# Eight k pairs instead of six in seven-product quads, with the first weight sum made by a negated copy and two adding transfers

## The chip, the core and the metric

The kernel runs on one core of a Trainium2 chip. Its engines are named here as the profile names them: PE (TensorE, matmul), PEld (TensorE's weight loads, which overlap PE), DVE (VectorE), ACT (ScalarE), POOL (GpSimd) and SP (SyncE, which issues most of the loads). The metric is the device time of one execution in microseconds; lower is better.

## The reference

One block of a network on 256 tokens of width 2048, in float32. It has three residual branches in a row: a gated feed-forward, a mixer (a recurrent RWKV part and a pooling part), and a second gated feed-forward. The change touches only the last matmul of the two feed-forwards.

```python
def _rmsnorm(x, g):
    y = x * lax.rsqrt(jnp.mean(x * x, axis=-1, keepdims=True) + NORM_EPS)
    return y * g

def _swiglu(x, w_gate, w_up, w_down):
    return (jax.nn.silu(x @ w_gate) * (x @ w_up)) @ w_down

f = _swiglu(_rmsnorm(h, ln_ffn1_pre), ffn1_gate, ffn1_up, ffn1_down)
h = h + 0.5 * _rmsnorm(f, ln_ffn1_post)
h = h + _rmsnorm(_hybrid_mixer(...), ln_mix_post)
f = _swiglu(_rmsnorm(h, ln_ffn2_pre), ffn2_gate, ffn2_up, ffn2_down)
h = h + 0.5 * _rmsnorm(f, ln_ffn2_post)
```

The down product `@ w_down` takes 256 x 5632 hidden values to 256 x 2048.

## The kernel before, in words

**Precision.** Every float32 operand is split in a rounded high part and a low part (`xH`, `xL` for activations, `wH`, `wL` for weights). One product of two blocks is three matmuls, in `mm3` (lines 156 to 160): high by high, low by high, high by low. A weight tile is 128 rows by 1024 values; ACT rounds it to `wH` (a cast) and DVE subtracts to get `wL`.

**Buffers.** A loaded tile `w32` has four buffers (`W32_BUFS`), `wH` and `wL` have five each (`WS_BUFS`). All larger temporary tiles share 33 units of 128 x 1024 values (`NUNITS`, `unit`, line 82). During a down product the 22 hidden activation tiles hold 22 of these units.

**The down product.** K is 5632, which is 44 blocks of 128 rows; the 2048 output columns are four chunks of 512. `post` (line 530) calls `seven` (line 235) twice per feed-forward, each time for two neighbouring chunks, called first (`cf`) and last (`cl`); so there are four calls in the kernel. Tokens are two halves of 128. A pair of neighbouring k blocks, two halves of tokens and two chunks of columns form a 2 x 2 by 2 x 2 product of blocks. In the plain form this takes eight products.

**Plain pairs.** `pair` (line 265) loads two k blocks of one chunk, 512 KB, splits them and makes four products. The call first runs over the plain pairs for the first chunk, then over those for the last one.

**Quads.** The first `NQ` = 6 k pairs, k blocks 0 to 11, are not done in the plain form, but each as one quad with seven products (`quad`, line 271; a Winograd form of Strassen's method). It needs sums of activation blocks and of weight blocks:

- `sums` (line 211) works on one activation tile, which covers two k pairs. DVE rebuilds x from `xH` and `xL` (the tile `sx`), makes four sums of its quarters (the tile `sf`), ACT rounds all four in one cast (`sH`, line 230) and DVE subtracts (`sL`, line 231). The results are kept and serve both calls of a feed-forward. The first `sums` stands ahead of the plain pairs; later ones are made inside the quads of the first call, ahead of need.
- The weights of a quad are loaded in two tiles `va` and `vb`, as four 256 KB transfers issued by SP (line 279). DVE makes the first weight sum, `t13`, as `va` minus a block of `vb` (line 283), and from it the two halves of `t24` (lines 285 and 286). In the trace both sums are called `t`. Four splits (lines 293 and 294) then give the high and low parts.

The seven products go to banks `p1`, `p5`, `p6`, `p7` (called `ms` in the trace) and `f0`, `l0`, `l1` (called `mm`). After the last quad `merge` (line 320) combines the four `ms` banks, and the first chunk is given out to be scaled and squared.

**Where the quads stand.** `QUADS` gives the plain pairs, counted from 0, behind which a quad is placed: for the first call (`False`) and the second one (`True`), each for the first chunk's pairs and the last chunk's. In the second call the last 16 k blocks of the last chunk are done token half by token half (`by_half`), so that one half can be finished while the other still computes.

**What sets the order.** A planner puts each engine's instructions in a fixed order by priority and by its own estimate of when their inputs are ready. Weight work is raised in priority (`high_priority` with `BOOST`). `sums` is not raised. At run time every engine and every queue works in that order, so an instruction that waits holds up all behind it. SP's queue issues the weight loads; POOL's queue issues the few other transfers around a down product: the broadcast gain `gb` (line 547), the residual (`xr` in the first feed-forward, `h` in the second, line 1297) and the spills.

**Just ahead of the first quad.** The last block of the up product ends in `shuffle_split` (line 485): sixteen ACT copies of 32 x 256 (line 493), a cast (line 496) and a DVE subtraction (line 497) give the last hidden tile.

Of the kernel before, what the change touches and what calls it, by code (L numbers as in the profile page):

```python
# [11 lines left out]
F32 = mybir.dt.float32  # L12
F32R = mybir.dt.float32r
AF = mybir.ActivationFunctionType
ALU = mybir.AluOpType
# [3 lines left out]
P = 128  # L19
# [24 lines left out]
TURNS = [[4.2, 5.3, 6.4, 7.5], [5.3, 6.0, 6.7, 7.4]]  # L44
WARM = 12
TB = 4
NQ = 6
QUADS = {False: ((4, 9, 14), (2, 5, 8)), True: ((2, 5, 8, 11, 14), (1,))}

ROWS = [("ln_mix_pre", 16), ("ln_ffn2_pre", 16), ("mu", 26), ("w0", 8), ("a0", 8),  # L50
        ("k_k", 8), ("k_a", 8)]
# [3 lines left out]
class Block:  # L55
# [41 lines left out]
    def at(s, t, fn):  # L97

        s.n += 1
        heapq.heappush(s.events, (t, s.n, fn))  # L100
# [109 lines left out]

    def sums(s, T, out):

        nc = s.nc
        V = nc.vector
        xH, xL = T[len(out) // 2]
        x = s.unit((P, 2, 2, S), F32, "sx")
        fl = lambda t: t.rearrange("p a b t -> p (a b t)")
        V.tensor_tensor(out=fl(x), in0=xH.bitcast(F32).rearrange("p k t -> p (k t)"),  # L218
                        in1=xL.bitcast(F32).rearrange("p k t -> p (k t)"), op=ALU.add)
        a11, a21 = x[:, :, 0, :P], x[:, :, 0, P:]  # L220
        a12, a22 = x[:, :, 1, :P], x[:, :, 1, P:]
        f = s.unit((P, 4, 2, P), F32, "sf")
        V.scalar_tensor_tensor(out=f[:, 0], in0=a21, scalar=-1.0, in1=a22, op0=ALU.mult,
                               op1=ALU.subtract)
        V.scalar_tensor_tensor(out=f[:, 1], in0=f[:, 0], scalar=-1.0, in1=a11,
                               op0=ALU.mult, op1=ALU.subtract)
        V.tensor_tensor(out=f[:, 2], in0=a11, in1=a21, op=ALU.subtract)
        V.tensor_tensor(out=f[:, 3], in0=a12, in1=f[:, 1], op=ALU.subtract)
        fH, fL = [s.unit((P, 4, 2, P), F32R, n_) for n_ in ("sH", "sL")]
        nc.scalar.copy(fl(fH), fl(f))  # L230
        V.tensor_tensor(out=fl(fL), in0=fl(f), in1=fl(fH).bitcast(F32), op=ALU.subtract)
        for i in range(2):
            out.append([(fH[:, m, i], fL[:, m, i]) for m in range(4)])

    def seven(s, w, cf, cl, at, KT, T, sm, ev_first, ev_last, trail):


        nc = s.nc
        V = nc.vector
        n = NQ  # L240
        K0 = 2 * n

        bank = {}
        for b in ("f0", "f1", "l0", "l1"):
            bank[b] = s.pm.tile([P, 512], F32, tag="mm", name=s.nm("mm"))
        for b in ("p1", "p5", "p6", "p7"):
            bank[b] = s.psum("ms")
        std = KT - K0
        left = dict(f0=std + n, f1=std, l0=std + n, l1=std + n, p1=n, p5=n, p6=n, p7=n)
        new = set(bank)  # L250

        def mul(b, x, wt):
            left[b] -= 1
            s.mm3(bank[b], *x, *wt, b in new, left[b] == 0)
            new.discard(b)

        def rows(k, h):
            xH, xL = at(k)
            return xH[:, h * P:h * P + P], xL[:, h * P:h * P + P]
        ws = {}  # L260

        def keep(tiles):
            ws.update((k, (wH, wL)) for k, wH, wL in tiles)

        def pair(k, c0, b):
            keep(s.load_w(w, k, 2, c0, 512))
            for i in range(2):
                for h in range(2):
                    mul(f"{b}{h}", rows(k + i, h), ws[k + i])

        def quad(q):
            k = 2 * q
            if len(sm) < min(q + 2, n):
                s.sums(T, sm)
            va, vb = [s.wp.tile([P, 1024], F32, tag="w32", name=s.nm("w32"), bufs=W32_BUFS)
                      .rearrange("p (a c) -> p a c", a=2) for _ in range(2)]
            for dst, kk, c0 in ((va[:, 0], k, cl), (vb[:, 0], k, cf), (va[:, 1], k + 1, cf),
                                (vb[:, 1], k + 1, cl)):
                nc.sync.dma_start(out=dst, in_=w[kk * P:kk * P + P, c0:c0 + 512])
            t13 = s.unit((P, 2, 512), F32, "t13")  # L280
            t24 = s.unit((P, 2, 512), F32, "t24")
            with s.tc.high_priority(offset=BOOST):
                V.tensor_tensor(out=t13, in0=va,  # L283
                                in1=vb[:, :1].to_broadcast([P, 2, 512]), op=ALU.subtract)
                V.tensor_tensor(out=t24[:, 0], in0=va[:, 0], in1=t13[:, 1], op=ALU.add)
                V.tensor_tensor(out=t24[:, 1], in0=vb[:, 1], in1=t24[:, 0], op=ALU.subtract)  # L286

            def split(v, m):
                wH = s.wp.tile([P, 1024], F32R, tag="wH", name=s.nm("wH"), bufs=WS_BUFS)
                wL = s.wp.tile([P, 1024], F32R, tag="wL", name=s.nm("wL"), bufs=WS_BUFS)  # L290
                H, L = [t_[:, :m * 512].rearrange("p (a c) -> p a c", a=m) for t_ in (wH, wL)]
                with s.tc.high_priority(offset=BOOST):
                    nc.scalar.copy(H, v)  # L293
                    V.tensor_tensor(out=L, in0=v, in1=H.bitcast(F32), op=ALU.subtract)  # L294
                return [(H[:, i], L[:, i]) for i in range(m)]
            s1, s2, s3, s4 = sm[q]
            b11, b22 = split(va, 2)
            mul("p1", rows(k, 0), b11)
            mul("f0", s4, b22)
            b21, = split(vb[:, 1:], 1)  # L300
            mul("l0", rows(k + 1, 0), b21)
            t1, t3 = split(t13, 2)
            mul("p5", s1, t1)
            mul("p7", s3, t3)
            t2, t4 = split(t24, 2)
            mul("p6", s2, t2)
            mul("l1", rows(k + 1, 1), t4)

        if not sm:
            s.sums(T, sm)  # L310
        q = iter(range(n))
        stop = KT - (TRAIL if trail else 0)
        for i, k in enumerate(range(K0, KT, 2)):
            pair(k, cf, "f")
            if i in QUADS[trail][0]:
                quad(next(q))
        tiles = list(range(K0, stop, 2))
        u = [s.tmp("u") for _ in range(4)]

        def merge():  # L320
            with s.tc.high_priority(offset=BOOST):
                nc.scalar.copy(u[0], bank["p1"])
                for o, b, i in ((1, "p6", 0), (2, "p7", 1), (3, "p5", 2), (1, "p5", 1),
                                (1, "f0", 1), (3, "f1", 3)):
                    V.tensor_tensor(out=u[o], in0=bank[b], in1=u[i], op=ALU.add)
                ev_first(0, u[1])
                ev_first(1, u[3])

        def finish(h):
            o = u[2 * h]  # L330
            V.tensor_tensor(out=o, in0=bank[f"l{h}"], in1=o, op=ALU.add)
            ev_last(h, o)
        for i, k in enumerate(tiles):
            pair(k, cl, "l")
            if i in QUADS[trail][1]:
                quad(next(q))
                if left["p1"] == 0:
                    merge()
        if not trail:
            with s.tc.high_priority(offset=BOOST):  # L340
                finish(0)
                finish(1)
            return
        s.now = 0.0
        s.by_half(w, cl, stop, KT, 0.0, AHEAD[0],
                  lambda k, h: mul(f"l{h}", rows(k, h), ws[k]), keep, finish)
# [1007 lines left out]
```

## Time and profile before

| | us |
|---|---|
| median of three runs | 2102.93 (2102.6 to 2103.97) |
| the profiled execution | 2103.1 |
| its span, first to last instruction | 2101.4 |
| PE busy | 2077.6 |
| DVE busy | 1389.0 |
| ACT busy | 1157.0 |
| POOL busy | 76.0 |
| bytes moved | 406.99 MB |
| mean granted TensorE clock | 0.994 |
| down product of the first feed-forward | about 490 to 720 |
| down product of the second | about 1850 to 2085 |

A group or an instruction in the trace is written as line, engine, operation and output <- inputs; numbers in square brackets are the idle time of the engine just before it and what ended that. A matmul over 512 columns is shown as 0.39 us long, since its end overlaps the next one; back to back they start 0.2267 us apart at full clock. So it is the starts that tell the rate.

### The profile page before, as it was taken

Reading aid. Unit: us, or ns where it says so; the run is one execution under the profiler, and the core shown is the slowest. Engines: PE = TensorE matmul, PEld = TensorE weight load, DVE = VectorE, ACT = ScalarE, POOL = GpSimd, SP = SyncE. Lnnn points to the kernel's source line nnn. Section 1 sums busy time; section 2 is a strip of 40 time slices with the busy share of each in tenths; the row PEclk is TensorE's granted clock in tenths of the full one; section 3 lists DMA queues with packets and bytes.
Section 4 is the critical chain, followed back from the end, with each engine's and each line's share of the span. In section 5 each row is a group of like instructions: output and inputs, shape, how many; then the busy total and the mean of one; then the engine's idle time right before and its main releaser. Section 6 shows DMA issues by size and latency. Waiting matters only on the chain.

```text
span 2101.4 us, 29096 instructions
## 1 busy us (share of the span) xinstructions
PE 2077.6 (99%) x11017; PEld 1748.1 (83%) x11017; DVE 1389.0 (66%) x1776; ACT 1157.0 (55%) x1658; POOL 76.0 (4%) x161
## 2 busy tenths in 40 slices
PE   9999999999999999999999999999999999989998
PEld 7888888887888899999888788888888888878886
DVE  6555555556787765799688666575655555567776
ACT  7565555655555565474466444466555565555543
POOL 0000000000000010000110110010000000000000
PEclk9999999999999999999999999999999999999999
DMA  7656666564667666556456565565665656645674
GB/s 260 194 179 208 194 194 196 178 204 153 207 196 253 222 188 189 177 165 194 133 159 189 160 249 188 194 220 181 197 203 191 192 179 208 195 152 199 205 243 160
DMA packets 224885, 406.99 MB, mean 194 GB/s; under 512 B 13919, under 2 KB 49897, under 8 KB 224745
## 3 DMA queue, kind: packets, MB, share of 16 engines
q1 hardware_dynamic: 218569, 384.69, 57.3%
q0 software_dynamic: 5888, 19.93, 2.6%
q8 instruction: 86, 1.41, 0.3%
q10 hardware_dynamic: 288, 0.52, 0.1%
q14 instruction: 54, 0.44, 0.1%
HBM read 396.69 MB, written 8.39 MB: 193 GB/s over the span
## 4 chain that ended last, share of the span: by engine, by line
PE 95%; DVE 2%; issue 1%; ACT 1%; POOL 0%; DMA 0%; POOLq 0%; DVEq 0%; SPq 0%; ACTq 0%
PE mm L158 26%; PE mm L160 26%; PE mm L159 26%; PE mc L438 10%; PE ms L159 1%; PE ms L160 1%; PE ms L158 1%; ACT x L493 1%; PE tr L466 1%; PE pA L1075 0%; ACT wH L293 0%; PE pSa L1183 0%; DVE sx L218 0%; PE pU L1171 0%; DMA w<-in_ffn_gate_dram 0%
## 5 line engine op out<-in xcount | busy, mean ns | idle before, releaser
L135 DVE TENSOR_TENSOR wL<-w,wH 128x1024 fp32r<-128x1024 f32 (+2 forms) x677 | 811.0, 1209 | 546.2 <-ACT wH L134 542.9
L134 ACT CAST wH<-w 128x1024 fp32r<-128x1024 f32 (+2 forms) x677 | 698.7, 1044 | 634.2 <-PE mm L160 491.9
L160 PE MATMUL mm<-wH,xL 128*128 128x512 f32 x2316 | 902.2, 390 | 0.7 <-DVE xL L474 0.7
L159 PE MATMUL mm<-wL,xH 128*128 128x512 f32 x2316 | 902.0, 389 | 0.0
L158 PE MATMUL mm<-wH,xH 128*128 128x512 f32 x2316 | 897.9, 392 | 0.0
L160 PEld LDWEIGHTS mm<-wH,xL 128*128 128x128 f32 x2316 | 435.1, 188 | 92.4 <-DVE xL L474 1.5
L158 PEld LDWEIGHTS mm<-wH,xH 128*128 128x128 f32 x2316 | 435.7, 188 | 90.3 <-ACT xH L472 0.2
L159 PEld LDWEIGHTS mm<-wL,xH 128*128 128x128 f32 x2316 | 435.4, 188 | 89.5 <-DVE wL L135 0.2
L438 PE MATMUL mc<-xH,wH 128*128 128x256 f32 x560 | 159.5, 285 | 0.0
L438 PE MATMUL mc<-xL,wH 128*128 128x256 f32 x560 | 158.4, 283 | 0.0
L438 PE MATMUL mc<-xH,wL 128*128 128x256 f32 x560 | 158.3, 283 | 0.0
L493 ACT COPY x<-T 32x256 f32<-32x256 f32 x352 | 141.9, 403 | 3.9
L438 PEld LDWEIGHTS mc<-xH,wH 128*128 128x128 f32 x560 | 106.0, 189 | 1.1
L438 PEld LDWEIGHTS mc<-xH,wL 128*128 128x128 f32 x560 | 106.0, 189 | 0.2
L438 PEld LDWEIGHTS mc<-xL,wH 128*128 128x128 f32 x560 | 106.0, 189 | 0.1
L293 ACT CAST wH<-t 128x1024 fp32r<-128x1024 f32 x48 | 50.5, 1051 | 63.0 <-DVE t L286 31.0
L293 ACT CAST wH<-w 128x1024 fp32r<-128x1024 f32 (+1 forms) x48 | 40.2, 838 | 63.7 <-DMA w<-in_ffn_down_dram 45.6
L294 DVE TENSOR_TENSOR wL<-t,wH 128x1024 fp32r<-128x1024 f32 x48 | 58.6, 1222 | 21.3 <-ACT wH L293 21.1
L294 DVE TENSOR_TENSOR wL<-w,wH 128x1024 fp32r<-128x1024 f32 (+1 forms) x48 | 44.7, 953 | 13.6 <-ACT wH L293 13.6
L283 DVE TENSOR_TENSOR t<-w,w 128x1024 f32<-128x1024 f32 x24 | 29.4, 1225 | 27.7 <-DMA w<-in_ffn_down_dram 26.6
L547 POOL DMA_DIRECT2D gb<-in_ln_ffn_post_dram x4 | 2.4, 592 | 1228.2 <-DVE wL L294 1228.2
L512 ACT ACTIVATE sg<-mm,rs 128x512 f32<-128x512 f32 x44 | 29.9, 689 | 22.5 <-PE mm L160 22.4
(284 smaller groups left out, 1510.4 us busy)
## 6 DMA issues: line engine op xcount, KB each, us to landing
w<-in_ffn_up_dram SPq DMA_DIRECT2D x176, 512.0 KB
w<-in_ffn_gate_dram SPq DMA_DIRECT2D x174, 512.0 KB
w<-in_ffn_down_dram SPq DMA_DIRECT2D x128, 512.0 KB
w<-in_w_in_dram SPq DMA_DIRECT2D x128, 512.0 KB
w<-in_ffn_down_dram SPq DMA_DIRECT2D x96, 256.0 KB
w<-in_w_out_dram SPq DMA_DIRECT2D x32, 512.0 KB
w<-in_w_proj_b_dram SPq DMA_DIRECT2D x16, 512.0 KB
w<-in_w_proj_a_dram SPq DMA_DIRECT2D x16, 512.0 KB
```

The lines of the kernel that those rows point to most:

```text
L134: s.nc.scalar.copy(vH, v)
L135: s.nc.vector.tensor_tensor(out=vL, in0=v, in1=vH.bitcast(F32), op=ALU.subtract)
L158: nc.tensor.matmul(ps, aH, bH, start=start, stop=False)
L159: nc.tensor.matmul(ps, aH, bL, start=False, stop=False)
L160: nc.tensor.matmul(ps, aL, bH, start=False, stop=stop)
L283: V.tensor_tensor(out=t13, in0=va, in1=vb[:, :1].to_broadcast([P, 2, 512]), op=ALU.subtract)
L293: nc.scalar.copy(H, v)
L294: V.tensor_tensor(out=L, in0=v, in1=H.bitcast(F32), op=ALU.subtract)
L438: s.nc.tensor.matmul(o, lh, rh, start=one and n == 0, stop=k == KT - 1 and n == 2, skip_group_check=True)
L466: nc.tensor.transpose(ps[:, i], src[:, i * P:(i + 1) * P], s.ident)
L493: nc.scalar.copy(dst[q * 32:q * 32 + 32, :, :, i], src[i * 32:i * 32 + 32, :, :, q])
L512: nc.scalar.activation(out=sg, in_=ps, func=AF.Sigmoid, scale=rs[h])
```

## The change

Five things change.

1. `NQ` goes from 6 to 8: k blocks 0 to 15 are done in quads, 28 k blocks in plain pairs.
2. `QUADS` places them anew. In the first call the first quad stands behind the seventh plain pair instead of the fifth, and the next ones follow after two or three pairs. In the second call they stand behind every second pair instead of every third.
3. `t13` is no longer a DVE subtraction. ACT copies the block of `vb` with a factor of -1 to both halves, and two transfers issued by POOL add the two blocks of `va` from HBM onto it (`accum_op`). `t24` is made from it by DVE as before.
4. The activation sums are split in three steps instead of one: the first two sums together, then the fourth, then the third, each with an ACT copy and a DVE subtraction.
5. They are kept in other places: the first two sums of two activation tiles share a unit, the fourth sums of all eight pairs share one, and the third overwrites a part of the activation tile itself that no later product reads. So eight pairs take six units, as six did before.

```diff
-NQ = 6
-QUADS = {False: ((4, 9, 14), (2, 5, 8)), True: ((2, 5, 8, 11, 14), (1,))}
+NQ = 8
+QUADS = {False: ((6, 8, 11, 13), (2, 4, 7, 9)), True: ((1, 3, 5, 7, 9, 11, 13), (1,))}
...
-        xH, xL = T[len(out) // 2]
+        j = len(out) // 2
+        xH, xL = T[j]
...
-        fH, fL = [s.unit((P, 4, 2, P), F32R, n_) for n_ in ("sH", "sL")]
-        nc.scalar.copy(fl(fH), fl(f))
-        V.tensor_tensor(out=fl(fL), in0=fl(f), in1=fl(fH).bitcast(F32), op=ALU.subtract)
+        if j % 2 == 0:
+            s.s12 = [s.unit((P, 2, 2, 2, P), F32R, n_) for n_ in ("sH", "sL")]
+        if j == 0:
+            s.s4 = [s.unit((P, NQ // 2, 2, P), F32R, n_) for n_ in ("sH", "sL")]
+        s12 = [u[:, j % 2] for u in s.s12]
+        s3 = [u.rearrange("p (i b) t -> p i b t", b=2)[:, :, 0, P:] for u in (xH, xL)]
+        s4 = [u[:, j] for u in s.s4]
+        for (H, L), v in ((s12, f[:, :2]), (s4, f[:, 3]), (s3, f[:, 2])):
+            nc.scalar.copy(H, v)
+            V.tensor_tensor(out=L, in0=v, in1=H.bitcast(F32), op=ALU.subtract)
         for i in range(2):
-            out.append([(fH[:, m, i], fL[:, m, i]) for m in range(4)])
+            out.append([(s12[0][:, 0, i], s12[1][:, 0, i]), (s12[0][:, 1, i], s12[1][:, 1, i]),
+                        (s3[0][:, i], s3[1][:, i]), (s4[0][:, i], s4[1][:, i])])
...
-                V.tensor_tensor(out=t13, in0=va,
-                                in1=vb[:, :1].to_broadcast([P, 2, 512]), op=ALU.subtract)
+                nc.scalar.activation(out=t13, in_=vb[:, :1].to_broadcast([P, 2, 512]),
+                                     func=AF.Copy, scale=-1.0)
+                for i, c0 in ((1, cf), (0, cl)):
+                    kk = k + i
+                    nc.gpsimd.dma_start(out=t13[:, i], in_=w[kk * P:kk * P + P, c0:c0 + 512],
+                                        accum_op=ALU.add)
                 V.tensor_tensor(out=t24[:, 0], in0=va[:, 0], in1=t13[:, 1], op=ALU.add)
                 V.tensor_tensor(out=t24[:, 1], in0=vb[:, 1], in1=t24[:, 0], op=ALU.subtract)
```

## The prediction

> **What bounds the kernel now.** I read the page's first part, then the waits of TensorE, then both stretches around them as windows, and last the order of instructions in one stretch.
>
> ```profile
> PE 2077.6 (99%) x11017; PEld 1748.1 (83%) x11017; DVE 1389.0 (66%) x1776; ACT 1157.0 (55%) x1658; POOL 76.0 (4%) x161
> ...
> PE ms L158 <- ACT wH L293: 5.7, 4, 1.8
> PE mm L158 <- ACT sH L230: 4.2, 2, 2.1
> ```
>
> TensorE has work for 99% of the span, so time falls only with matmuls or with its few waits. After the first line (busy us, share, instructions) come lines of the table of waits (us in total, times, longest): the two longest TensorE has, both in the down products, on split weights (L293) and split activation sums (L230).
>
> ```profile
> 505.00:518.00 13.00, 7.91 (x18) 4.83 (x18) 11.82 (x17) 7.05 (x8) 0.00 (x0) 0.61 0.30 83
> 598.00:690.00 92.00, 92.00 (x407) 76.20 (x406) 71.91 (x76) 47.98 (x56) 2.68 (x5) 1.00 0.71 232
> 1865.50:1880.00 14.50, 8.86 (x22) 5.88 (x21) 13.32 (x19) 8.07 (x8) 0.00 (x0) 0.65 0.30 107
> ```
>
> Windows: length, then busy time of PE, PEld, DVE, ACT, POOL, then granted clock, DMA share, GB/s. The first and third are the first quad of each feed-forward: TensorE partly idle and at a clock of 0.61 and 0.65. The second is the other five quads of the second column pair: TensorE full, VectorE at 78%, ScalarE at 52%.
>
> ```profile
> 504.77 0.39 PE L160 MATMUL mm<-wH,xL 128*128 128x512 f32 x1
> 507.25 0.55 PE L158 MATMUL mm<-wH,sH 128*128 128x512 f32 x1 [2.09 <-ACT sH L230]
> 507.60 0.63 PE L159 MATMUL mm<-wL,sH 128*128 128x512 f32 x1
> 508.51 0.80 PE L160 MATMUL mm<-wH,sL 128*128 128x512 f32 x1 [0.28 <-DVE sL L231]
> 510.78 1.22 PE L158 MATMUL ms<-wH,sH 128*128 128x512 f32 x2 [1.47 <-ACT wH L293]
> ...
> 502.17 1.23 DVE L497 TENSOR_TENSOR xL<-x,xH 128x1024 fp32r<-128x1024 f32 x1 [0.26 <-ACT xH L496]
> 503.31 1.22 DVE L218 TENSOR_TENSOR sx<-xH,xL 128x1024 f32<-128x1024 f32 x1
> ...
> 507.23 1.22 DVE L231 TENSOR_TENSOR sL<-sf,sH 128x1024 fp32r<-128x1024 f32 x1 [1.11 <-ACT sH L230]
> 508.37 1.22 DVE L283 TENSOR_TENSOR t<-w,w 128x1024 f32<-128x1024 f32 x1
> ```
>
> The activation sums start (503.31) only behind the last block's split (502.17), because ScalarE's sixteen block copies run from 493.9 to 500.5 and VectorE waits behind them. The first weight sum (L283) follows at 508.37, though its loads were issued by 487.9. Undisturbed matmuls start 0.2267 us apart. From 504.99 to 517.97 only 16 start, worth 3.63 us: 9.35 us lost. In the second feed-forward 20 start between 1865.58 and 1880.09 (4.53 us): 9.97 lost. Together 19.3 us, of which some 10.7 are idle and the rest slow clock.
>
> **The change, part by part.** *Two more pairs per call.* A pair of k blocks costs eight products in plain form and seven in a quad; each is three matmuls. Four calls by two more quads by 3 x 0.2267 = 0.68 us: minus 5.4 us, wherever TensorE stays full.
>
> *The first weight sum.* Per quad, VectorE loses one subtraction of 1.22 us (L283). ScalarE gets a copy with factor -1 over 128x1024; the nearest row is its cast of the same size, 1.05 us. POOL gets two issues; its gb issues take 0.54 to 0.70 us, measured beside a busy VectorE, so 1.2 us. Per quad 512 KB more are moved, 16.8 MB in all on 407 MB. ScalarE then works about 6.9 of a 10.2 us cycle (two plain pairs 5.44, quad 4.76): two casts, 3.77 of quad casts, 1.05. VectorE works 7.9 of it. Both stay hidden as work; what counts is latency. Queued behind: on ScalarE the casts of that sum and all later weights; on VectorE L285 and L286, which free the load buffers SyncE waits for (it already waits on L286 12 times). On POOL gb and the residual loads share the queue with the new transfers; nothing is due there until the merge.
>
> *What the two transfers take, from issue to both landed.* No row shows an adding transfer. Nearest rows:
>
> ```profile
> h<-hsp POOLq DMA_DIRECT2D x8, 512.0 KB, 12.5
> gb<-in_ln_ffn_post_dram POOLq DMA_DIRECT2D x4, 512.0 KB, 4.1
> xr<-in_x_dram POOLq DMA_DIRECT2D x4, 512.0 KB, 6.7
> ...
> w<-in_rwkv_g_dram POOLq DMA_DIRECT2D x2, 256.0 KB, 3.0
> ```
>
> Below: 3.0 for one 256 KB load plus a second issue of 0.55, 3.6 us. Above: 12.5. The rows from this stage with the same bytes are gb (4.1) and xr (6.7, four in a row); the destination is read as well, so I take between them, 5.5 us. The Trainium skill, "DMA: Bandwidth & Descriptors", section "Anatomy of one DMA", has a transfer at 2.0 us plus bytes over 436 GB/s, an estimate of 2.6 us for each of these and so some 3.2 for both; "Collectives: The Full Stack", section "The bandwidth ceiling", says that a reducing transfer is slower because it needs two source reads, not because of its adder. By the first alone the dense quads below would cost nothing; no run here shows either.
>
> *The first quad later.* It moves by two pairs, 5.44 us. Its first product would start at 509.07, the one with s4 by 509.75, p5 at 511.1. The sums still hang on the last block: one 1.05 cast stands where a 0.62 one stood, so sx starts near 503.9, the fourth sum is done near 506.7, and the three copies (0.62, 0.4, 0.4) and subtractions (0.69, 0.42, 0.42) end near 508.4, that of s4 near 508.0. So the wait on sums, 2.1 us, goes. Next late is the first weight sum. If the negated copy comes behind the sums, as L283 does now, it is 508.0 + 1.05 + 0.3 of hand-over + 5.5 = 514.9, its cast 516.0, and TensorE waits 4.9 us at p5, about what it idles today (5.1): no gain. If it runs once its loads have landed (near 493), the sum is ready at 500 and there is no wait: all 19.3 us gained. The trace doesn't settle which; nothing puts it nearer one end, so I take half: plus 9.8 us gained.
>
> On the clock: the matmul after the 2.09 us wait already goes at 0.35 and the rest at 0.43, so a stall here costs about its double. The Trainium skill, "TensorE: Matmul & The Clock Gate", section "Part 1: The HAM clock gate", drops the clock only after an idle window of about 3.4 us; by it the half-wait of 2.45 us would cost itself alone, some 2.4 us less per feed-forward. The row differs, and I go by the row.
>
> *The sums.* Three splits in place of one, four times rather than three per feed-forward, add some 5 us of VectorE and 2.5 of ScalarE; behind the first quad they lie beside full matmuls: nothing on the path. The third sum's halves go into the activations' own tile, at rows that no later product reads: nothing.
>
> *Dense quads.* In the second pair the cycle shrinks from 12.9 (three pairs and a quad) to 10.2 us. Two loops must fit it. The sum's own unit: copy 1.05, transfers 5.5, cast 1.05, subtraction 1.22, hand-overs 0.6: 9.4, with two units free until the fourth quad (33, less 22 of activations, 6 of sums, 3 of output). The four load buffers: the two plain loads hold some 6.5 us each, va and vb about 4 to land + 0.3 + 1.05 + 0.3 + 5.5 + 1.4 = 12.5 each, 38 buffer-us over 4 buffers, 9.5 us. Both fit by under a microsecond. Today's margin is 3 to 6 us a quad (the fifth quad's t24 is cast by 661.63 and used at 665.32), which takes up jitter. I take 1.5 us lost per feed-forward: plus 3. Ends: zero, and with slow transfers the rival below.
>
> **Sum.** 2103.1 (this execution: span 2101.4 and 1.7 around it) - 5.4 - 9.8 + 3 = 2090.9. The median of the three runs, 2102.93, is the same within 0.2: I forecast 2091.
>
> **Rivals.** *The sum arrives in time everywhere.* For it: loads lie ready 15 us before the first quad, and instructions can be ordered around the transfers. Against: L283 was ready as early and still ran at 508. Time: 2103.1 - 5.4 - 19.3 = 2078.4.
>
> *The wait only changes its name.* The first quad waits on the sum as long as now: 2103.1 - 5.4 + 3 = 2100.7, within 0.2%. For it: the 508.37 row. Against: TensorE's order can put the next two pairs, 5.4 us of work, before p5.
>
> *Slow transfers make the loop the bound (slower).* With L for the transfers, the unit's loop is 3.9 + L. At 12 cycles above 10.2 us, less 3 us of lead per feed-forward, the loss is 12 (L - 6.3) - 6. At L = 7.7 it eats the 5.4 and about 5 still gained at the first quad; above that the kernel is slower. At L = 9 the loss is 26 and the first quad gains nothing: 2103.1 - 5.4 + 26 = 2124. For it: xr 6.7 and h 12.5, and the extra read; the same stage already moves 232 GB/s. Against: gb 4.1 to land there.
>
> **How the numbers follow.** Forecast 0.42, own range 2084 to 2098 (first quad wait between a quarter and three quarters of today's, dense loss 0 to 6). In time everywhere 0.20. Wait renamed 0.13. Slow transfers 0.25. A difference under 0.2% (4.2 us) is about what a measurement here can't tell from none. Faster is the first two, 0.62; same 0.12; slower 0.26. The range takes the first three whole, from 2077, and the slow case up to 2118 (L near 8.5); about 0.16 lies outside.
>
> **What would show it.** Right: 24 matmuls fewer on TensorE (8 quads by 3); the wait on L230's successor gone; the window of the first quad with a clock above 0.8; a clock of 1.00 in the second pair; landings of 4 to 7 us in the new transfer rows. Wrong: waits of TensorE on casts of t13 in every quad of the second pair, VectorE idle before L285 until a DMA, a clock under 1.00 there, or landings over 8 us.

## The result, and the profile after

The changed kernel takes 2219.36 us (median of four runs, 2214.99 to 2222.06) against 2102.89 of the kernel before beside it: 1.0551 times as long, with an interval of 1.0531 to 1.057. The forecast was 2091, the range ended at 2118. The profiled execution took 2221.2 us with a span of 2219.5.

First the page of the changed kernel: its span, the busy time of each engine, the chain that ended last by engine, and the new transfers that POOL issues in the down products (number, size, median us from issue to landing).

```profile
span 2219.5 us, 29390 instructions
...
PE 2118.2 (95%) x10993; PEld 1760.2 (79%) x10993; DVE 1393.0 (63%) x1812; ACT 1193.5 (54%) x1724; POOL 132.5 (6%) x225
...
PE 73%; DMA 12%; ACT 5%; issue 5%; DVE 3%; POOL 1%; SPq 0%; ACTq 0%; POOLq 0%; DVEq 0%
...
t<-in_ffn_down_dram POOLq DMA_DIRECT2D x64, 256.0 KB, 6.4
```

TensorE has the 24 matmuls fewer that were forecast (11017 to 10993), but it has work for only 95% of a longer span, and transfers hold 12% of the chain (the new ones 9%), where the page of before had 0%. The waits of the changed kernel (us in total, times, longest):

```profile
ACT wH L307 <- DMA t<-in_ffn_down_dram: 190.7, 26, 9.0
DVE t L299 <- DMA t<-in_ffn_down_dram: 148.4, 32, 5.9
PE ms L158 <- ACT wH L307: 87.6, 50, 6.3
...
SPq L289 <- DVE t L299: 176.1, 22, 11.9
```

The new transfers are waited for in three places at once. ScalarE waits to cast `t13` (L307), VectorE waits in each of the 32 quads to make `t24` (L299), and SyncE's queue holds the next quad's loads (L289) until the first half of that `t24` is made, since it frees their buffers. TensorE's waits on sum casts went from 5.7 to 87.6 us. The same windows as before, in the same columns (length; busy time of PE, PEld, DVE, ACT, POOL; granted clock; DMA share; GB/s):

```profile
505.00:520.00 15.00, 8.71 (x36) 6.62 (x35) 10.00 (x18) 4.93 (x7) 1.97 (x2) 0.87 0.47 113
...
598.00:690.00 92.00, 81.12 (x317) 63.36 (x316) 56.30 (x62) 43.24 (x53) 11.15 (x13) 0.91 0.70 190
```

The window from 598 to 690 held 407 matmuls before and holds 317 now, and VectorE (71.91 to 56.30) and ScalarE (47.98 to 43.24) are *less* busy than before; the DMA engines move 190 GB/s in place of 232. No engine has become the bound; something takes turns. One turn of it, a steady quad of the second call (start, duration, engine, line, out <- inputs, and in brackets the idle time before and what ended it):

```profile
665.12 0.69 DVE L300 TENSOR_TENSOR t<-w,t 128x512 f32<-128x512 f32 x1
665.16 1.78 SPq L289 DMA_DIRECT2D w<-in_ffn_down_dram  x4
665.88 1.99 ACT L307 CAST wH<-t 128x1024 fp32r<-128x1024 f32 x2 [8.51 <-DVE t L300]
667.78 1.99 ACT L134 CAST wH<-w 128x1024 fp32r<-128x1024 f32 x2
...
669.67 1.04 ACT L307 CAST wH<-w 128x1024 fp32r<-128x1024 f32 x1
...
670.62 1.05 ACT L293 ACTIVATE t<-w 128x1024 f32<-128x1024 f32 x1
...
671.96 1.76 POOL L297 DMA_DIRECT2D t<-in_ffn_down_dram  x2 [13.05 <-ACT t L293]
679.23 0.69 DVE L299 TENSOR_TENSOR t<-w,t 128x512 f32<-128x512 f32 x1 [5.90 <-DMA t<-in_ffn_down_dram]
...
679.99 1.78 SPq L289 DMA_DIRECT2D w<-in_ffn_down_dram  x4
680.55 1.99 ACT L307 CAST wH<-t 128x1024 fp32r<-128x1024 f32 x2 [8.37 <-DMA t<-in_ffn_down_dram]
```

The loads of a quad are issued at 665.16. Its negated copy starts 5.46 us later, behind five casts of ScalarE that themselves begin only once the quad before has its sums. The copy takes 1.05, the hand-over 0.29; the transfers, from their first issue to the start of `t24`, 7.27 (that start needs only the first of the two; the cast of `t13` needs both and starts at 680.55); `t24`'s first half 0.76 with its hand-over. At 679.99 the next quad's loads are issued, and the turn begins again. 5.46 + 1.05 + 0.29 + 7.27 + 0.76 = 14.83 us, and the next quad's loads leave only behind this quad's second sum. TensorE's work for the same stretch is 10.2 us.

### The profile page after: what moved, and what is told of

Its sections match the earlier page's. It is cut to its first block, busy times and chain, and to the rows that moved or that the text cites. A ratio compares the mean times of both kernels' runs of the same rounds, so it can differ in the third digit from the quotient of the medians.

```text
span 2219.5 us, 29390 instructions
## 1 busy us (share of the span) xinstructions
PE 2118.2 (95%) x10993; PEld 1760.2 (79%) x10993; DVE 1393.0 (63%) x1812; ACT 1193.5 (54%) x1724; POOL 132.5 (6%) x225
## 4 chain that ended last, share of the span: by engine, by line
PE 73%; DMA 12%; ACT 5%; issue 5%; DVE 3%; POOL 1%; SPq 0%; ACTq 0%; POOLq 0%; DVEq 0%
PE mm L158 20%; PE mm L160 20%; PE mm L159 20%; PE mc L452 9%; DMA t<-in_ffn_down_dram 9%; DMA w<-in_ffn_down_dram 3%; ACT wH L307 2%; ACT t L293 1%; ACT wH L134 1%; DVE wL L308 1%; DVE wL L135 1%; PE tr L480 1%; ACT x L507 1%; POOL t L297 0%; PE pA L1089 0%
## 5 line engine op out<-in xcount | busy, mean ns | idle before, releaser
L135 DVE TENSOR_TENSOR wL<-w,wH 128x1024 fp32r<-128x1024 f32 (+2 forms) x661 | 790.6, 1209 | 533.6 <-ACT wH L134 532.1
L134 ACT CAST wH<-w 128x1024 fp32r<-128x1024 f32 (+2 forms) x661 | 680.3, 1043 | 603.3 <-PE mm L160 447.3
L159 PE MATMUL mm<-wL,xH 128*128 128x512 f32 x2268 | 885.0, 390 | 0.0
L160 PE MATMUL mm<-wH,xL 128*128 128x512 f32 x2268 | 884.6, 390 | 0.0
L158 PE MATMUL mm<-wH,xH 128*128 128x512 f32 x2268 | 883.4, 395 | 0.0
L307 ACT CAST wH<-t 128x1024 fp32r<-128x1024 f32 x64 | 64.3, 1044 | 234.2 <-DMA t<-in_ffn_down_dram 190.7
L297 POOL DMA_DIRECT2D t<-in_ffn_down_dram x64 | 56.6, 1040 | 1359.2 <-ACT t L293 1295.7
L158 PE MATMUL ms<-wH,sH 128*128 128x512 f32 x64 | 39.1, 612 | 87.6 <-ACT wH L307 87.6
L299 DVE TENSOR_TENSOR t<-w,t 128x512 f32<-128x512 f32 x32 | 22.2, 692 | 148.4 <-DMA t<-in_ffn_down_dram 148.4
L158 PEld LDWEIGHTS ms<-wH,sH 128*128 128x128 f32 x64 | 14.5, 227 | 115.0 <-ACT wH L307 114.8
L308 DVE TENSOR_TENSOR wL<-t,wH 128x1024 fp32r<-128x1024 f32 x64 | 76.2, 1222 | 32.5 <-ACT wH L307 32.4
L308 DVE TENSOR_TENSOR wL<-w,wH 128x1024 fp32r<-128x1024 f32 x64 | 59.5, 953 | 10.1 <-ACT wH L307 10.0
```

Source lines behind the costliest of these rows:

```text
L134: s.nc.scalar.copy(vH, v)
L135: s.nc.vector.tensor_tensor(out=vL, in0=v, in1=vH.bitcast(F32), op=ALU.subtract)
L158: nc.tensor.matmul(ps, aH, bH, start=start, stop=False)
L159: nc.tensor.matmul(ps, aH, bL, start=False, stop=False)
L160: nc.tensor.matmul(ps, aL, bH, start=False, stop=stop)
L297: nc.gpsimd.dma_start(out=t13[:, i], in_=w[kk * P:kk * P + P, c0:c0 + 512], accum_op=ALU.add)
```

## The experiments

All times are medians. "After" is the changed kernel.

**Which part costs it.** The first four runs undo or single out the new way to the first weight sum.

*Subtraction again.* Eight quads, new places, the first sum by VectorE as before:

```diff
-                nc.scalar.activation(out=t13, in_=vb[:, :1]..., func=AF.Copy, scale=-1.0)
-                for i, c0 in ((1, cf), (0, cl)):
-                    nc.gpsimd.dma_start(out=t13[:, i], in_=w[...], accum_op=ALU.add)
+                V.tensor_tensor(out=t13, in0=va,
+                                in1=vb[:, :1].to_broadcast([P, 2, 512]), op=ALU.subtract)
```

> The changed kernel with the first weight sum made by VectorE's subtraction again; eight quads, their new places and the split sums stay. Latency theory (each quad waits for the two adding transfers, and ScalarE's and VectorE's queues stand behind that wait): the 87.6 us of TensorE waits on casts of the sum go, 5.4 us of products are saved and some of the first quad's 19.3 us: 2080 to 2098 us. Density theory (quads behind every second pair ask more of the load buffers or of VectorE than these give): TensorE still waits in every quad, over 2150 us.

Measured: 2123.79 us, 1.0101 [1.0086, 1.0116], between the two expectations. So 96 of the 117 us are the copy and the transfers. What is left is still slower than before.

*Copy and one VectorE addition.* After, with the two transfers replaced by one VectorE instruction:

```diff
-                for i, c0 in ((1, cf), (0, cl)):
-                    nc.gpsimd.dma_start(out=t13[:, i], in_=w[...], accum_op=ALU.add)
+                V.tensor_tensor(out=t13, in0=va, in1=t13, op=ALU.add)
```

> The changed kernel with ScalarE's negated copy kept, and one VectorE addition of 1.2 us in place of the two transfers. Latency theory: within 6 us of the form with VectorE's subtraction alone. If the copy's place in ScalarE's queue is what costs: over 2150 us.

Measured: 2101.05 us, 0.999 [0.998, 0.9999]. The two transfers alone make 118 us of difference. It also beats the subtraction, by 23 us where at most 6 were expected, with the same VectorE busy time (1426 us in both). By the trace the difference is order: the subtraction is one instruction that needs its loads, and it stands ahead of the plain pairs' subtractions (L135), as in this stretch of VectorE in the run with the subtraction:

```profile
636.25 1.23 DVE L293 TENSOR_TENSOR t<-w,w 128x1024 f32<-128x1024 f32 x1 [1.01 <-DMA w<-in_ffn_down_dram]
637.39 2.35 DVE L135 TENSOR_TENSOR wL<-w,wH 128x1024 fp32r<-128x1024 f32 x2
```

With the copy, ScalarE has the first wait for those loads, and VectorE's addition comes after. In the run with the subtraction TensorE's matmuls wait 17 times for L135, 11.8 us in total; the run with the copy and the addition lists no such wait. The order was not varied by itself. One turn of the kernel with the VectorE addition:

```profile
660.40 2.60 SPq L289 DMA_DIRECT2D w<-in_ffn_down_dram  x4
...
666.29 1.06 ACT L293 ACTIVATE t<-w 128x1024 f32<-128x1024 f32 x1
...
669.61 0.69 DVE L296 TENSOR_TENSOR t<-w,t 128x512 f32<-128x512 f32 x1
...
670.37 2.60 SPq L289 DMA_DIRECT2D w<-in_ffn_down_dram  x4
```

It is the same ring (loads, copy, first sum, second sum, loads), closed in the same way, but 9.97 us long: just under TensorE's 10.2.

*The copy and transfers alone*, in the kernel before, six quads in their old places (the reverse of the first diff):

> The kernel before with only the first weight sum changed to the negated copy and the two adding transfers; six quads at their old places, behind every third to fifth pair. Latency theory with a fixed price per quad: the changed kernel loses (2219 - 2091) / 32 = 4.0 us a quad, so 24 quads cost some 96 us: 2185 to 2205 us. Buffer-loop theory (a quad's loads wait for the sums of the quad before, a loop of some 15.5 us): the quads five pairs apart (18.4 us of TensorE work) lose nearly nothing and only those three pairs apart (12.9 us) lose some 2.6 us: 2120 to 2150 us. Density theory without the transfers: about 2103 us.

Measured: 2169.11 us, 1.0313 [1.0297, 1.0328], between the two expectations. Dense quads are not needed for the loss. In the second call, with 12.9 us of TensorE work a quad, the quads' loads are issued every 15.4 to 15.6 us (652.09, 667.47, 683.11, 698.72). In the first call (first feed-forward, from one start of POOL's issues to the next) the two turns over five pairs, 18.4 us of TensorE work, take 20.9 and 18.8, the one over four pairs (15.6) takes 18.6, and the two over three (12.9) take 15.4 and 15.6. So there is a floor of some 15 us a quad, and the wider turns lose something as well.

*Plain transfers.* After, with the transfers overwriting the copy in place of adding to it:

```diff
-                    nc.gpsimd.dma_start(out=t13[:, i], in_=w[...], accum_op=ALU.add)
+                    nc.gpsimd.dma_start(out=t13[:, i], in_=w[...])
```

> The changed kernel with plain transfers in place of the adding ones: the same bytes, queue, order and waits, but the subtraction is left out, so the weight sums are not those of the product. If it is the adding that makes the transfers long: they land in some 3.5 us rather than 6.4, and the time falls to 2100 to 2140 us. If it is the way through POOL's queue beside the weight loads, or just one more dependent transfer: they still land in over 5.5 us, and the time stays over 2180 us.

Measured: 2165.49 us, 1.03 [1.0285, 1.0315], between the two expectations. So 54 of the 118 us belong to the addition in the transfer, 64 to any transfer there. The plain ones land in 4.7 us (median) and POOL issues one in 0.546 us; the adding ones need 6.4 and 0.986.

**Can the ring be opened?** Two causes fit so far: ScalarE's order (the next copy stands behind casts that wait for the transfers) and the load buffers (held until `t24` is made).

*Ahead.* After, with a quad cut in two: loads, copy and transfers are called two plain pairs ahead of the rest.

```diff
-        def quad(q):
+        def ahead(q):
...
+            parts.append((q, k, va, vb, t13, t24))
+
+        def quad():
+            q, k, va, vb, t13, t24 = parts.pop(0)
...
+            if i + 1 in QUADS[trail][0]:
+                ahead(next(q))
             pair(k, cf, "f")
             if i in QUADS[trail][0]:
-                quad(next(q))
+                quad()
```

> The changed kernel with each quad cut in two: its loads, negated copy and adding transfers are placed two plain pairs ahead of its products, the rest stays. Serial-loop theory (on ScalarE the copy for the next quad stands behind the casts that wait for this quad's transfers, so copy, transfers and casts follow one another, 14.8 us a cycle where TensorE has 10.2 us of work): now they run beside two plain pairs, and only the reuse of the sum's unit, some 11 to 12.5 us, is left: 2115 to 2160 us. Rate theory (the adding transfers can't go faster than one pair in some 14 us, whatever the order): over 2200 us.

Measured: 2191.6 us, 1.0421 [1.0404, 1.0439]: 28 us better than after, between the two expectations, and no cure. The copy now waits for its loads in 23 of the 32 quads (64.6 us in total, up to 5.1), which wait for buffers.

*Ahead, with plain transfers:*

> The form with loads, copy and transfers two pairs ahead, with plain transfers in place of the adding ones; the subtraction is left out, so the weight sums are not those of the product. The adding transfers held the transfer engines 351 engine-us for 3.67 MB where plain ones held them 159. If that is what keeps the early form at a cycle of 12 to 14.6 us and 2191.6 us: the cycle falls under 11 us and the time to 2105 to 2135 us. If it is the load buffers, held until the sums are made, whatever the kind of transfer: over 2155 us.

Measured: 2162.97 us, 1.0283 [1.0268, 1.0299], no better than plain transfers in the old order (2165.49), and where the second theory had put it (the load buffers).

*Second sum without va and vb.* After, so that `t24` no longer holds the load buffers:

```diff
-                V.tensor_tensor(out=t24[:, 0], in0=va[:, 0], in1=t13[:, 1], op=ALU.add)
-                V.tensor_tensor(out=t24[:, 1], in0=vb[:, 1], in1=t24[:, 0], op=ALU.subtract)
+                V.tensor_tensor(out=t24[:, 0], in0=t13[:, 0], in1=t13[:, 1], op=ALU.add)
+                V.tensor_tensor(out=t24[:, 1], in0=t13[:, 0], in1=t24[:, 0], op=ALU.subtract)
```

> The changed kernel, but the second weight sum (L299, L300) is made from the first alone, with as many instructions of the same size: it leaves out the two blocks that the second sum should read from va and vb. So the four load buffers no longer stay held until the two transfers have landed; they come free after their own casts and subtractions. The planner then places the next quad's copy two or three casts earlier in ScalarE's order, still behind the cast of the present quad's first sum. Theory 'two loops of one length' (the load buffers' and ScalarE's order, each some 14.8 us a quad today): what stays is ScalarE's, one to three casts (1 to 3 us) and a copy 1.05, hand-over 0.3, transfers 7.3, second sum 0.8, so 11 to 12.5 us a quad: 60 of 118 us come back, 2140 to 2175. Rival 'the load buffers alone': the quads' own work sets the pace again, 10.2 to 10.5 us in the second pair, 2100 to 2125. Rival 'ScalarE's order alone': the buffers were never the limit and only the moved copy counts, some 2 us a quad, 2185 to 2205.

Measured: 2214.49 us, 1.0529 [1.0511, 1.0547]: none of the three. SyncE's waits on `t24`, 176 us, were gone and the time stayed. VectorE's part of the trace suggests why:

```profile
662.93 0.69 DVE L299 TENSOR_TENSOR t<-t 128x512 f32<-128x512 f32 x1 [2.68 <-DMA t<-in_ffn_down_dram]
663.54 1.82 DVE L308 TENSOR_TENSOR wL<-w,wH 128x1024 fp32r<-128x1024 f32 x2
```

The subtractions of `va` and `vb` (L308) are the next readers of those buffers, and in VectorE's fixed order they stand behind the instruction that waits for the transfer. In this stretch the buffers still came free only behind the transfer; the name of the wait had changed.

*Both at once* (ahead, and the second sum without va and vb):

> Both at once: the quad cut in two with loads, copy and adding transfers two plain pairs ahead (as in the run named early), and the second weight sum made from the first alone, so that no load buffer waits for a transfer; the two blocks of va and vb are again left out of that sum. Theory 'two loops': with both loosened the loop is the sum's own unit (copy 1.05, 0.3, transfers 5 to 7.3, two sums 1.4, cast) with two units, so it no longer binds: 10.2 to 11 us a quad, 2100 to 2130, near the kernel with the copy and an addition on VectorE (2101). Rival 'ScalarE's order alone': what the early placing gave is all there is, 2185 to 2195. Rival 'the transfers' own contention with the loads': the buffers free, but casts still wait for loads that land late, 2145 to 2175.

Measured: 2203.24 us, 1.0479 [1.0463, 1.0495], worse than "ahead" alone and outside all three ranges. Again VectorE did `t24` ahead of those subtractions.

*VectorE's order turned too.* As the last one, but the second sum reads the low part of `vb`, so it can only come behind the two subtractions:

```diff
-                V.tensor_tensor(out=t24[:, 0], in0=t13[:, 0], in1=t13[:, 1], op=ALU.add)
...
+            b21, = split(vb[:, 1:], 1)
+                V.tensor_tensor(out=t24[:, 0], in0=b21[1].bitcast(F32), in1=t13[:, 1], op=ALU.add)
```

> As the run that has the quad cut in two and the second weight sum made without va and vb, but that sum now reads the low part of vb, so that VectorE must do the two subtractions that free va's and vb's buffers ahead of the sum that waits for the transfers (it leaves out the two weight blocks of the second sum, as before, and adds a low part instead). Theory 'waits at the head of the queues': loads no longer hang on a transfer; what is left is one ScalarE loop of copy 1.06, hand-over 0.3, transfers 7.3, cast 1.05 = 9.7 us, below TensorE's 10.2: 10.2 to 11 us a quad in the second pair, 2100 to 2135. Rival 'the transfers hold back the loads': the casts still wait for loads that land late, 12 to 13 us a quad, 2165 to 2205.

Measured: 2182.99 us, 1.0369 [1.0348, 1.039]. And with plain transfers:

> The same with plain transfers in place of the adding ones (so the first weight sum's subtraction is left out as well; same bytes). Theory 'waits at the head of the queues': the loop falls by some 2.5 us to 7.2 and binds nowhere: 2095 to 2115, no more than 20 below the run with adding transfers. Rival 'the transfers hold back the loads': the plain ones hold the DMA engines 2.2 times shorter, so 2130 to 2165, well below the adding ones.

Measured: 2157.4 us, 1.0253 [1.0238, 1.0268]. Both lie where the rival had put them (transfers that hold back the loads). But in these two traces casts wait for late loads for another reason than in the changed kernel: the quad's loads, asked for early, keep two of the four load buffers through the two plain pairs (with adding transfers, loads issued at 669.47 are last read from 681.94 on). So they don't decide it, and no run here opened the ring: which of its links holds it, the load buffers or ScalarE's order, was not separated.

**Time in the ring, or load on the DMA engines?** In place of the two adding transfers of 256 KB, two small plain ones of 16 KB, the second behind the landing of the first:

```diff
-                for i, c0 in ((1, cf), (0, cl)):
-                    kk = k + i
-                    nc.gpsimd.dma_start(out=t13[:, i], in_=w[kk * P:kk * P + P, c0:c0 + 512],
-                                        accum_op=ALU.add)
+                for _ in range(2):
+                    nc.gpsimd.dma_start(out=t13[:, :, :16], in_=w[k * P:k * P + P, cf:cf + 32]
+                                        .rearrange("p (a c) -> p a c", a=2))
```

> The changed kernel; in place of the two adding transfers of 256 KB, two plain ones of 16 KB (128 rows by two strips of 16 values), the second behind the first's landing since both write the same place. The addition is left out, so t13 is only the negated copy with a wrong strip. Nearest row: 64 KB loads by POOL land in 2.6 us; with an issue of about 0.5 each and a hop, some 5 to 5.7 us for both. Theory 'one serial loop': the loop is 7.6 + 5.3 = 12.9 us a quad. Two measured points give the line: plain transfers, loop 12.3, 64 us above the kernel without transfers; adding ones, 14.83, 118 us above: 21 us per us of loop. So 2101 + 77 = 2178, 2160 to 2195. Rival 'load on the DMA engines': 32 KB a quad instead of 512 KB load nothing, 2100 to 2125.

Measured: 2206.23 us, 1.0487 [1.0469, 1.0504]. With three in a row:

> The same with three small transfers, each behind the landing of the one before (the addition is left out again). Theory 'one serial loop': some 7.5 to 8.5 us for the three, so a loop of 15.1 to 16.1 us a quad: 2101 + 118 + 21 x (0.3 to 1.3), 2215 to 2255, as slow as the adding transfers or slower, with 48 KB a quad. Rival 'load on the DMA engines': 2100 to 2130.

Measured: 2288.5 us, 1.0884 [1.0868, 1.0901]. That decides against the load: 48 KB a quad, a tenth of the changed kernel's 512 KB, and it is slower by 69 us. Time in the ring is enough for a loss of this size; what the load of the large transfers adds beyond their own length was not separated. A turn of the ring with two small transfers:

```profile
673.45 1.78 SPq L289 DMA_DIRECT2D w<-in_ffn_down_dram  x4
...
678.61 1.05 ACT L294 ACTIVATE t<-w 128x1024 f32<-128x1024 f32 x1
679.96 0.72 POOL L297 DMA_DIRECT2D t<-in_ffn_down_dram  x1 [8.80 <-ACT t L294]
683.19 0.72 POOL L297 DMA_DIRECT2D t<-in_ffn_down_dram  x1 [2.51 <-DMA t<-in_ffn_down_dram]
...
685.50 0.69 DVE L299 TENSOR_TENSOR t<-w,t 128x512 f32<-128x512 f32 x1 [4.60 <-DMA t<-in_ffn_down_dram]
...
686.26 1.78 SPq L289 DMA_DIRECT2D w<-in_ffn_down_dram  x4
```

Five kernels with the quads in the same places, one turn of each in the second call in us (from the starts of the rows named above; the first half of `t24` and the hand-over to SyncE are in "rest"), and the mean of the six turns from the second to the eighth quad's loads in that call:

| first sum by | loads to copy | copy | to second sum | rest | turn | mean turn | kernel |
|---|---|---|---|---|---|---|---|
| VectorE addition | 5.89 | 1.06 | 2.26 | 0.76 | 9.97 | 10.24 | 2101.05 |
| two plain transfers | 5.37 | 1.05 | 4.84 | 0.77 | 12.03 | 12.27 | 2165.49 |
| two small in a row | 5.16 | 1.05 | 5.84 | 0.76 | 12.81 | 13.58 | 2206.23 |
| two adding transfers | 5.46 | 1.05 | 7.56 | 0.76 | 14.83 | 14.49 | 2219.36 |
| three small in a row | 5.40 | 1.05 | 8.89 | 0.76 | 16.10 | 16.05 | 2288.5 |

Of the four parts only "to second sum" differs by more than a microsecond, and the time follows it. In the kernel with the VectorE addition TensorE is busy for the whole turn; five of its six turns are 9.88 to 9.97 us, the last is 11.70. The size of the step did not come out as the expectations had it: they took 21 us of kernel time for one us of ring, and from the plain transfers to three small ones it is 123 / 3.78 = 33, uneven from row to row. Both expectations came out too low, by 11.2 us and 33.5 us at their upper ends.

**The first quad later, by itself.** In the kernel before, only the first call's places:

```diff
-QUADS = {False: ((4, 9, 14), (2, 5, 8)), True: ((2, 5, 8, 11, 14), (1,))}
+QUADS = {False: ((6, 10, 14), (2, 5, 8)), True: ((2, 5, 8, 11, 14), (1,))}
```

> The kernel before, with six quads and VectorE's sum, where only the first call's first three quads stand behind plain pairs 6, 10 and 14 instead of 4, 9 and 14. If the first quad's 9.4 us a feed-forward are lost because its sums come one after the other behind the last block, two more plain pairs (5.4 us) take most of that away: 2085 to 2092 us. If VectorE's whole work behind the last block is late and only moves along: 2097 to 2103 us.

Measured: 2096.72 us, 0.9967 [0.9956, 0.9979]: just below the second range, 6.6 us gained. Then two pairs later still, with (8, 11, 14):

> The kernel before (six quads, VectorE's sum) with the first call's quads behind plain pairs 8, 11 and 14, the first one two pairs later than in the form that took 2096.7 us. That form still waits 6.9 us at its first quads, for weight sums that VectorE makes behind the activation sums. If only their lateness costs, 5.4 us more of plain work cover it: 2084 to 2091 us. If VectorE's backlog moves along with the quad: 2094 to 2099 us.

Measured: 2086.93 us, 0.9921 [0.9905, 0.9938], the fastest kernel of this study. Of its waits, the one that was 5.7 us before:

```profile
PE ms L158 <- ACT wH L293: 1.2, 2, 0.6
```

The 16.5 us gained are most of the 19.3 that the prediction had counted as lost at the two first quads.

**Eight quads without transfers, spread better.** The kernel with copy and VectorE addition, first call at

```diff
-QUADS = {False: ((6, 8, 11, 13), (2, 4, 7, 9)), ...
+QUADS = {False: ((6, 9, 12), (1, 4, 6, 8, 10)), ...
```

> The form with ScalarE's copy and VectorE's addition, eight quads, with the first call's quads behind pairs 6, 9, 12 and 1, 4, 6, 8, 10: three plain pairs between the first five in place of two or three in turn. If VectorE (97% busy from 540 to 570 us in that form) is what keeps the saved products from showing: 2085 to 2097 us. If it is the second call or the first quad alone: 2099 to 2103 us.

Measured: 2098.33 us, 0.9977 [0.9967, 0.9986], between the two. And at ((8, 11, 13), (1, 4, 6, 8, 10)):

> Eight quads by ScalarE's copy and VectorE's addition, the first call's quads behind pairs 8, 11, 13 and 1, 4, 6, 8, 10. If the first quad's wait (5.4 us of idle TensorE with its slow clock in the form that took 2098.3 us) goes: 2086 to 2093 us. If VectorE's work for eight quads is the limit wherever they stand: 2096 to 2101 us.

Measured: 2094.45 us, 0.9958 [0.9943, 0.9973], just above the first range: with 24 matmuls fewer it stays 7.5 us behind the six-quad kernel with the same first quad. Between 500 and 620 VectorE is busy for 109.85 of 120 us and the window holds 498 matmuls; the six-quad kernel has 101.83 and 525. By these rows VectorE, at 92%, holds TensorE back there; that was not tried by itself.

## Why the prediction was wrong

**The step that failed is "Dense quads".** It set two loops beside TensorE's 10.2 us: the sum's own unit, 9.4, and the load buffers, "38 buffer-us over 4 buffers, 9.5 us", and took 3 us of loss. In place of two loops there is one. By the page, with 5.4 us of matmuls off and some 2 gained at the two first quads (below), this term measured 2221.2 - (2103.1 - 5.4 - 2) = 125.5 us.

By the trace, the average was the error. In the second call four loads a quad (`va`, `vb`, two plain pairs) go round through four buffers, so the buffer of one quad's `va` goes to the next quad's `va`, and a short hold of the plain loads lends it nothing: in the turn shown, the next quad's loads leave at 679.99, right behind `t24`'s first half (679.23 + 0.69). The prediction had the hold of `va` in its own numbers, 12.5 us, already above 10.2; divided out with the plain ones it looked like 9.5. The copy's place behind casts that wait for the quad before was left out too: 5.5 us from loads to copy against 4 + 0.3 there. The measured ring is 7.6 us plus the transfers, where the prediction's rival had 3.9 + L.

**The transfers' term** L was taken as 5.5 us from the first issue to both landed, between 3.6 and 12.5. In the turn shown both have landed 8.5 us after the first issue (7.7 in the median of the 32 quads); the ring itself has 7.27 of it, since `t24` starts on the first one. The term was mis-sized, but this did not decide: with the two small transfers the second sum starts 5.84 us after the copy's end, hand-over included, and the kernel takes 2206. By the rival's own formula 8.5 us would have cost 12 x (8.5 - 6.3) - 6 = 20 us. The sign of that rival came true with another mechanism. Nor are 12 turns touched but nearly all: the ring of 15 us lies above the 12.9 of quads three pairs apart as well. In the second call seven turns are 14.5 rather than 10.2, some 30 us; in the first, seven turns of about 15.5 stand against 79.5 us of matmuls, some 29; two feed-forwards make 118, the measured gap to the kernel with the VectorE addition.

**Two more pairs per call.** 24 matmuls fewer: right. The 5.4 us were given "wherever TensorE stays full", and it did not.

**The first quad later.** The wait on the activation sums went, as forecast, and the prediction's worse end for the first weight sum came true: the copy runs behind the sums' casts.

```profile
508.40 0.41 ACT L239 CAST xH<-sf 128x256 fp32r<-128x256 f32 x1 [3.56 <-DVE sf L229]
...
509.57 1.06 ACT L293 ACTIVATE t<-w 128x1024 f32<-128x1024 f32 x1
...
515.41 0.69 DVE L299 TENSOR_TENSOR t<-w,t 128x512 f32<-128x512 f32 x1 [4.97 <-DMA t<-in_ffn_down_dram]
...
518.39 0.79 PE L158 MATMUL ms<-wH,sH 128*128 128x512 f32 x1 [6.29 <-ACT wH L307]
```

The prediction gave 4.9 us of waiting for that branch; it is 6.29 here and 6.16 in the second feed-forward. From 505 to 524 TensorE starts 45 matmuls, worth 10.20 us, so 8.80 are lost against 9.35 before. From 1926 to 1946 it starts 52, worth 11.79 us, so 8.21 are lost against 9.97. Together some 2 us are gained. The wait of 6.29 us cost 8.80 in all, so a stall here cost 1.4 times itself and not its double. Half of 19.3 was the wrong middle of two ends: this part was the rival "the wait only changes its name". With six quads and VectorE's sum the same move by two pairs is worth 6.6 us, and one by four pairs 16.5.

**The pieces.** ScalarE's copy takes 1.057 us, taken as 1.05. POOL needs 1.76 us for the two issues, taken as 1.2. Nothing on the path for the smaller sums: nothing against it in the trace.

**The signs named ahead.** Waits of TensorE on casts of `t13`, VectorE idle ahead of the second sum (L285 then, L299 now) until a transfer, and a clock under 1.00 in the second pair (0.91): all three stood for "wrong" and are there. Landings of 4 to 7 us stood for "right", and the median is 6.4 (4.3 to 9.4). The missing wait on the activation sums and the first quad's clock above 0.8 (0.87 from 505 to 520, 0.82 up to 524) stood for "right" too and are there, though 8.80 us are lost at that quad. A time of landing said nothing without the ring it stands in.

## What to carry to other kernels

When a transfer is put between two engines, write down the whole ring from one use of a buffer to its next: load, place in each engine's queue, work, transfer, last reader. If loads per turn equal the number of buffers, the bound is the longest hold and not the mean. An instruction that waits for a transfer holds all behind it on its engine, those that free buffers too; taking one wait out of the table, even its longest, gains nothing where another instruction in the same order waits for the same thing. Try the smallest part of a change alone: here the later first quad, one line, is worth 6.6 us with the two pairs of the change and 16.5 us with four, and no run shows a gain from the rest.

## What the runs showed of the hardware

An adding transfer costs more than a plain one of the same bytes on every count: 0.986 against 0.546 us to issue on POOL, 6.4 against 4.7 us to land. The queue that carries them, in the second pair of the changed kernel (packets, MB, share of 16 engines over 105 us):

```profile
q0 software_dynamic: 2016, 3.67, 20.9%
```

and in the kernel with plain transfers (over 85 us):

```profile
q0 software_dynamic: 1120, 3.67, 11.7%
```

That is 351 against 159 engine-us (share times 16 times the window) for the same 3.67 MB: 2.2 times. The Trainium skill, "Collectives: The Full Stack", section "The bandwidth ceiling", puts the price of ReduceScatter's adding in its two source reads; the 2.2 times of engine time here fit that, though no run parts the second read from the addition. The Trainium skill, "DMA: Bandwidth & Descriptors", section "Anatomy of one DMA", gave an estimate of 2.6 us for one 256 KB transfer. The 16 KB ones, at 2.3 us, lie near its fixed part of 2.0, but beside the weight loads the 256 KB ones took 4.7 plain and 6.4 adding.

What stays open: whether more load buffers would open the ring at eight quads with adding transfers. It was not tried.
